# Feed-forward products of a two-layer encoder as seven block products instead of eight, with weight sums on GpSimd

## The chip, the cores and the metric

The kernel runs on one core of a Trainium2 chip. The metric is the device time of one execution in microseconds (us); three executions of the kernel before were timed. TensorE (PE) multiplies matrices out of SBUF into the banks of PSUM (8 banks of 128 x 512 float32), VectorE (DVE), ScalarE (ACT) and GpSimd (POOL) work elementwise, and the queue of SyncE (SP) issues loads. Each engine runs its own instructions in their order and waits on semaphores for the others.

## What is computed

Two layers of an encoder over 512 tokens of 1024 features. Each layer has a feed-forward at half weight, three token mixers in parallel with one output projection, and a second feed-forward:

```python
D_MODEL = 1024; SEQ = 512; DEPTH = 2; D_FF = 2816

def swiglu(x, wg, wu, wd):
    return (jax.nn.silu(x @ wg) * (x @ wu)) @ wd

for l in range(DEPTH):
    x = x + 0.5 * swiglu(rms_norm(x, ffn1_norm[l]), ffn1_wg[l], ffn1_wu[l], ffn1_wd[l])
    h = rms_norm(x, mix_norm[l])
    ...                                   # differential, dilated and latent attention on h @ w_in[l]
    x = x + mix @ w_o[l]
    x = x + 0.5 * swiglu(rms_norm(x, ffn2_norm[l]), ffn2_wg[l], ffn2_wu[l], ffn2_wd[l])
```

All inputs are float32. The change touches the four feed-forwards, and with them how x is held.

## The kernel before

**Products.** Every float32 operand is split in two parts of the type float32r: the high part `hi` is a rounded copy made by ScalarE (L69), the low part `lo` is what is left, made by VectorE (L70: the raw tile less the high part, both in SBUF). A product is three matmuls (`mm3`, L81 to L83): hi x hi, hi x lo, lo x hi.

**Layout.** x is held with features on partitions (`xT`, eight tiles of 128 x 512). A feed-forward splits x times the norm's gain into `xg` (eight pairs of tiles, L72 and L73); the token factor of the norm is applied behind the products, as a row `rb` that L200 makes.

**Feed-forward.** The 2816 hidden features are 22 columns of 128, taken in groups of 2, 4, 4, 4, 4, 4 (`FF_GROUPS`). `gate_up` (L232) makes one column: 24 matmuls for the gate into a bank of A, 24 for the up part into a bank of B, each with a 128 x 128 weight as the stationary and 512 tokens as the moving operand. VectorE and ScalarE make silu(gate) x up of them (L245 to L250) and split it. `down` (L256) multiplies a group by the rows of `wd`, eight times 12 matmuls into banks of D, and adds half of each to x (L264). The down products of a group are issued between the columns of the next group. Weights come through SP's queue into two `raw` tiles of 8 KB a partition (tag `raw`, `N_RAW` = 2), high and low parts into four tiles each (`N_W` = 4).

**POOL** adds the squares for the norm at each border (L184, L186), makes powers (L98) and works in the mixers (L442, L802).

**Order.** The program's text gives an order; a scheduler places the instructions of each engine but SP by its own estimate, so neighbouring columns mix on PE and DVE. SP's loads stay in the order of the text (`manual_schedule`).

## Time and profile before

| what | value |
|---|---|
| timed executions, median of 3 | 2065.02 us (2064.61 to 2065.61) |
| span of the profiled execution, first to last instruction | 2064.5 us |
| PE busy, share of the span | 98% |
| DVE, ACT, POOL busy | 58%, 42%, 18% |
| mean granted clock of PE, share of full | 0.997 |
| loads and stores, mean over the span | 93 GB/s |
| one feed-forward (1036 to 1398 us) | 362 us |
| one mixer (391 to 676 us) | 285 us |

How to read it: the profiled execution has its span as its own time, and the timed ones lie 0.1 to 1.1 us above it. A matmul's shown duration overlaps the next one's, so PE's pace is read from a stretch's length and count. An operation's duration on DVE or POOL includes time in which it is issued but can't go on. Busy shares are averages over stages; the stage tables say more.

### The profile page before, as it was taken

Reading aid. Unit: us, or ns where it says so; the run is one execution under the profiler, and the core shown is the slowest. Engines: PE = TensorE matmul, PEld = TensorE weight load, DVE = VectorE, ACT = ScalarE, POOL = GpSimd, SP = SyncE. Lnnn points to the kernel's source line nnn. Section 1 sums busy time; section 2 is a strip of 40 time slices with the busy share of each in tenths; the row PEclk is TensorE's granted clock in tenths of the full one; section 3 lists DMA queues with packets and bytes.
Section 4 is the critical chain, followed back from the end, with each engine's and each line's share of the span. In section 5 each row is a group of like instructions: output and inputs, shape, how many; then the busy total and the mean of one; then the engine's idle time right before and its main releaser. Section 6 shows DMA issues by size and latency. Waiting matters only on the chain.

```text
span 2064.5 us, 27177 instructions
## 1 busy us (share of the span) xinstructions
PE 2032.4 (98%) x10535; PEld 1732.5 (84%) x10535; DVE 1204.3 (58%) x2043; ACT 876.2 (42%) x1547; POOL 380.4 (18%) x442
## 2 busy tenths in 40 slices
PE   8999999999999999999999999999998999999999
PEld 6788888999888888888888888889997888888887
DVE  5544454678897655444555544455879985445444
ACT  5222232567876332222333222235779763223221
POOL 2100000444683100000010000005547630000000
PEclk9999999999999999999999999999999999999999
DMA  4632232421111233322323332234211022333322
GB/s 142 213 123 82 82 103 92 114 81 49 48 58 59 79 117 108 107 82 82 103 76 118 104 111 82 82 102 122 63 37 57 30 88 88 102 93 112 102 82 82
DMA packets 192689, 188.82 MB, mean 91 GB/s; under 512 B 8303, under 2 KB 187557, under 8 KB 192560
## 3 DMA queue, kind: packets, MB, share of 16 engines
q1 hardware_dynamic: 183200, 170.02, 26.5%
q10 hardware_dynamic: 7104, 11.27, 1.8%
q0 software_dynamic: 2256, 5.78, 0.9%
...
## 4 chain that ended last, share of the span: by engine, by line
PE 90%; DVE 4%; ACT 3%; DMA 2%; issue 1%; SPq 0%; ACTq 0%; POOL 0%; DVEq 0%; POOLq 0%
PE psA L83 12%; PE psA L81 12%; PE psA L82 12%; PE psB L82 8%; PE psB L81 8%; PE psB L83 8%; PE psD L81 7%; PE psD L83 7%; PE psD L82 7%; PE psD L810 2%; DMA raw<-in_ffn_wg_dram 2%; PE psE L839 1%; PE psE L830 1%; PE psC L429 1%; PE psB L505 1%; DVE wlo L70 1%
## 5 line engine op out<-in xcount | busy, mean ns | idle before, releaser
L69 ACT ACTIVATE whi<-raw 128x1024 fp32r<-128x1024 f32 (+3 forms) x448 | 362.8, 814 | 883.7 <-PE psB L82 287.8
L70 DVE TENSOR_TENSOR wlo<-raw,whi 128x1024 fp32r<-128x1024 f32 (+3 forms) x448 | 423.6, 948 | 119.7 <-ACT whi L69 110.5
L83 PE MATMUL psA<-xg,wlo 128*128 128x512 f32 x800 | 313.8, 392 | 3.5 <-DVE wlo L70 3.5
L81 PE MATMUL psA<-xg,whi 128*128 128x512 f32 x800 | 313.7, 392 | 1.6 <-ACT whi L69 1.6
L82 PE MATMUL psA<-xg,whi 128*128 128x512 f32 x800 | 312.6, 391 | 0.0
L82 PE MATMUL psB<-xg,whi 128*128 128x512 f32 x736 | 286.5, 389 | 0.0
L83 PE MATMUL psB<-xg,wlo 128*128 128x512 f32 x736 | 286.5, 389 | 0.0
L81 PE MATMUL psB<-xg,whi 128*128 128x512 f32 x736 | 286.5, 389 | 0.0
L81 PE MATMUL psD<-a,whi 128*128 128x512 f32 x704 | 274.4, 391 | 1.0 <-DVE xT L264 1.0
L83 PE MATMUL psD<-a,wlo 128*128 128x512 f32 x704 | 274.1, 389 | 0.0
L249 DVE TENSOR_TENSOR qk<-psB,o 128x512 f32<-128x512 f32 x88 | 60.8, 691 | 290.2 <-PE psB L83 290.2
L264 DVE SCALAR_TENSOR_TENSOR xT<-psD,xT 128x512 f32<-128x512 f32 x192 | 132.1, 690 | 142.4 <-PE psD L83 142.4
L184 POOL COPY o<-qk 128x512 f32<-128x512 f32 x5 | 4.2, 838 | 988.8 <-ACT qk L181 988.8
L83 PEld LDWEIGHTS psA<-xg,wlo 128*128 128x128 f32 x800 | 150.8, 188 | 37.3 <-DVE wlo L70 6.1
L81 PEld LDWEIGHTS psA<-xg,whi 128*128 128x128 f32 x800 | 151.0, 189 | 32.9 <-ACT whi L69 2.3
L82 PEld LDWEIGHTS psA<-xg,whi 128*128 128x128 f32 x800 | 150.9, 189 | 30.9
L81 PE MATMUL psA<-whi,xg 128*128 128x256 f32 (+2 forms) x592 | 173.8, 294 | 1.6 <-ACT xg L72 0.8
L82 PE MATMUL psA<-wlo,xg 128*128 128x256 f32 (+2 forms) x592 | 170.1, 287 | 0.0
L83 PE MATMUL psA<-whi,xg 128*128 128x256 f32 (+2 forms) x592 | 170.1, 287 | 0.0
L81 PEld LDWEIGHTS psB<-xg,whi 128*128 128x128 f32 x736 | 138.1, 188 | 28.9
L82 PEld LDWEIGHTS psB<-xg,whi 128*128 128x128 f32 x736 | 138.2, 188 | 28.6
L83 PEld LDWEIGHTS psB<-xg,wlo 128*128 128x128 f32 x736 | 138.1, 188 | 28.6
...
## 6 DMA issues: line engine op xcount, KB each, us to landing
...
```

Of the source, the lines that this page charges most:

```text
L69: nc.scalar.activation(hi, src, AF.Copy)
L70: eng.tensor_tensor(out=lo, in0=src, in1=hi.bitcast(F32), op=ALU.subtract)
L81: nc.tensor.matmul(o, ah, bh, start=(i == 0), stop=False)
L82: nc.tensor.matmul(o, ah, bl, start=False, stop=False)
L83: nc.tensor.matmul(o, al, bh, start=False, stop=(i == n - 1))
L249: nc.vector.tensor_tensor(out=tu, in0=pU, in1=rb[0], op=ALU.mult)
L264: nc.vector.scalar_tensor_tensor(out=xT[d], in0=pY, scalar=0.5, in1=xT[d], op0=ALU.mult, op1=ALU.add)
L429: nc.tensor.transpose(pt[:rows, t * P:(t + 1) * P], zsel(t), ident)
L505: nc.tensor.matmul(pS, qk[c, 0][:96, t * P:(t + 1) * P], qk[c, 1][:96, :], start=True, stop=True)
L810: nc.tensor.transpose(pT[:, kt * P:(kt + 1) * P], e[:, kt * P:(kt + 1) * P], ident)
L830: nc.tensor.matmul(hd.av[:, t * 64:(t + 1) * 64], pt[:, kt * P:(kt + 1) * P], hd.v(kt), start=(kt == 0), stop=(kt == NT - 1),)
L839: nc.tensor.matmul(o, hd.v(kt), x[:, :, kt, :], start=(i + kt == 0), stop=(i == 1 and kt == NT - 1))
```

## The change

The feed-forwards go by one Strassen level in Winograd's form. Tokens, the features summed over and the outputs are each cut in two, so a product of 2 x 2 blocks takes seven block products and sums in place of eight block products.

- x is held with tokens on partitions (`X`, eight tiles of 128 x 512). Stationary operands are now 128 tokens of x or of the hidden values, and weights are the moving operand, up to 512 columns wide. PE transposes x (`x_transposed`) and the hidden values (`hidden_operand`) into the operand's layout: 32 and 88 transposes in a feed-forward.
- For each 128 of the summed features the operand has eight pieces of 256 tokens: the blocks A11, A12, A21, A22 and four sums S1 to S4. `sums` makes the sums on POOL in three instructions (512, 256 and 256 elements), `split7` makes the high and low parts of seven pieces (1792 elements).
- An up block covers n columns (2, then five times 4). Its second operand is the gate's (11 and 21, by halves of the features) and the up part's weights (12 and 22). A down block is `wd` for the same n columns, cut by halves of columns and of outputs. `Seven` holds either. It loads eight raw tiles of 128 x 2 x 512 for an up block of four, four for a down block. POOL makes the four sums of weights: u1 = 11 + 12, then in place 12 + 22, u1 + 22 and 21 = (u1 + 22) + 21: for an up block of four two adds of 128x1024 each, for a down block one each.
- `run` issues seven products, below called first to seventh: (A11, 11) and (A12, 21) into banks of A, (S1, u1) into D, (S2, u1 + 22) and (S3, 12 + 22) into B, (S4, 22) on top of D, (A22, 21) into A. Each has two token tiles: for an up block of four 24 matmuls of 512 columns, for a down block 12. Between the products of a bank the sum so far is read by `done`: ScalarE copies q1, VectorE reads q6, q5 and the others out of PSUM; in a down block POOL adds q6 and q67 to x (three additions per token tile).
- Order of blocks: up 0, up 1, down 0, up 2, down 1, ... up 5, down 4, down 5. Behind the second product of up i come the transposes, sums and splits of the operand for down i - 1.
- The raw ring has ten tiles of 4 KB a partition. Mixers read x by transposes and add the output projection to it with tokens on partitions; its first half goes in 192 matmuls of 256 columns in place of 96 of 512. The store of x at the end needs no transposes.

The core of the diff (the mixers' adaptions and the readers of q1, q12 are left out):

```diff
-FF_GROUPS = (2, 4, 4, 4, 4, 4)
+FF_BLOCKS = (2, 4, 4, 4, 4, 4)
...
-    N_XG, N_A, N_RAW, N_W, N_QK = 16, 6, 2, 4, 8
+    N_XG, N_A, N_RAW, N_W, N_QK, N_T = 16, 6, 10, 4, 8, 5
...
+    X = [[cp.tile([P, H], F32, name=f"x{t}{d}") for d in range(2)] for t in range(NT)]
...
+    I_A11, I_A12, I_S2, I_S3, I_S1, I_S4, I_A22, I_A21 = range(8)
+    def sums(c, eng=nc.gpsimd):
+        eng.tensor_tensor(
+            out=c[:, I_S3:I_S1 + 1, :], in0=c[:, I_A21:I_A21 + 1, :].to_broadcast([P, 2, Q]),
+            in1=c[:, I_A11:I_A22 + 1:I_A22, :], op=ALU.subtract,
+        )
+        eng.tensor_tensor(out=c[:, I_S2, :], in0=c[:, I_A11, :], in1=c[:, I_S1, :], op=ALU.subtract)
+        eng.tensor_tensor(out=c[:, I_S4, :], in0=c[:, I_A12, :], in1=c[:, I_S2, :], op=ALU.subtract)
+    class Seven:
...
+        def add(self, dst, a, b):
+            for h in range(len(self.parts)):
+                if (dst, h) not in self.raw:
+                    self.raw[dst, h] = wraw([P, len(self.parts[h]), self.w])
+                nc.gpsimd.tensor_tensor(out=self.raw[dst, h], in0=self.raw[a, h], in1=self.raw[b, h], op=ALU.add)
+        def multiply(self, i, key, tag, start, stop):
+            w = []
+            for h, ks in enumerate(self.parts):
+                hi, lo = wsplit(self.raw[key, h], [P, len(ks), self.w])
+                w += [(hi[:, j, :], lo[:, j, :]) for j in range(len(ks))]
+            for t in range(2):
+                if start:
+                    self.banks[tag, t] = bank(tag)
+                tk = slice(t * P, (t + 1) * P)
+                mm3(
+                    self.banks[tag, t][:, :self.w], [(h[:, i, tk], lo[:, i, tk]) for h, lo in self.ops], w,
+                    start, stop,
+                )
+                yield t, self.banks[tag, t][:, :self.w]
+        def run(self, done):
+            self.add("u1", "11", "12")
+            for t, o in self.multiply(I_A11, "11", "A", True, False):
+                done("q1", t, o)
+            for t, o in self.multiply(I_A12, "21", "A", False, True):
+                done("q12", t, o)
+            self.add("12", "12", "22")
+            yield
+            for t, o in self.multiply(I_S1, "u1", "D", True, False):
+                done("q5", t, o)
+            self.add("u1", "u1", "22")
+            for t, o in self.multiply(I_S2, "u1", "B", True, False):
+                done("q6", t, o)
+            self.add("21", "u1", "21")
+            for t, o in self.multiply(I_S3, "12", "B", False, True):
+                done("q67", t, o)
+            for t, o in self.multiply(I_S4, "22", "D", False, True):
+                done("q53", t, o)
+            for t, o in self.multiply(I_A22, "21", "A", True, True):
+                done("q4", t, o)
...
+        def split7(op, c):
+            h, lo = op
+            nc.scalar.activation(h, c[:, :7, :], AF.Copy)
+            nc.vector.tensor_tensor(out=lo, in0=c[:, :7, :], in1=h.bitcast(F32), op=ALU.subtract)
...
-        def gate_up(m, raws, aT):
-            i = m % 2
-            c = slice(i * P, (i + 1) * P)
-            rg, ru = raws
-            gh, gl = wsplit(rg[:, :, c], [P, KD, P])
-            pG = bank("A")
-            mm3(pG, [(gh[:, k, :], gl[:, k, :]) for k in range(KD)], xg)
-            uh, ul = wsplit(ru[:, :, c], [P, KD, P])
-            pU = bank("B")
-            mm3(pU, [(uh[:, k, :], ul[:, k, :]) for k in range(KD)], xg)
...
-        def down(m0, gn, aT, final):
-            for dp in range(KD // 2):
-                rw = wload(wd[:, m0:m0 + gn, 2 * dp * P:2 * (dp + 1) * P], [P, gn, 2 * P])
...
-                    d = 2 * dp + i
-                    dh, dl = wsplit(rw[:, :, i * P:(i + 1) * P], [P, gn, P])
-                    pY = bank("D")
-                    mm3(pY, [(dh[:, j, :], dl[:, j, :]) for j in range(gn)], aT)
-                    nc.vector.scalar_tensor_tensor(
-                        out=xT[d], in0=pY, scalar=0.5, in1=xT[d], op0=ALU.mult, op1=ALU.add
-                    )
...
+                elif what == "q5":
+                    s["q5", t] = o
+                elif what == "q6":
+                    s["v", t] = hid[:, t, :w]
+                    nc.vector.tensor_tensor(out=s["v", t], in0=o, in1=s["q1", t][:, :w], op=ALU.subtract)
+                elif what == "q67":
+                    y = s["w", t] = s["q1", t][:, :w]
+                    nc.vector.tensor_tensor(out=y, in0=o, in1=y, op=ALU.subtract)
+                    nc.vector.tensor_tensor(out=hid[:, u, :w], in0=s["q5", t], in1=y, op=ALU.add)
+                elif what == "q53":
+                    y = hid[:, t, :w]
+                    nc.vector.tensor_tensor(out=y, in0=o, in1=y, op=ALU.add)
+                    nc.vector.scalar_tensor_tensor(
+                        out=y, in0=y, scalar=r[:, t:t + 1], in1=s["g", t][:, :w], op0=ALU.mult, op1=ALU.mult
+                    )
+                else:
+                    y = s["w", t]
+                    nc.vector.tensor_tensor(out=y, in0=o, in1=y, op=ALU.subtract)
+                    nc.scalar.activation(y, y, AF.Silu, scale=r[:, u:u + 1])
+                    z = hid[:, u, :w]
+                    nc.vector.scalar_tensor_tensor(
+                        out=z, in0=z, scalar=r[:, u:u + 1], in1=y, op0=ALU.mult, op1=ALU.mult
+                    )
...
+                elif what in ("q6", "q67"):
+                    y = tmp() if what == "q6" else s["q1", t]
+                    nc.vector.scalar_tensor_tensor(
+                        out=y, in0=o, scalar=0.5, in1=s["q1", t], op0=ALU.mult, op1=ALU.subtract
+                    )
+                    if what == "q6":
+                        nc.gpsimd.tensor_tensor(out=X[t][1], in0=X[t][1], in1=y, op=ALU.add)
+                    else:
+                        nc.gpsimd.tensor_tensor(out=X[u][1], in0=X[u][1], in1=y, op=ALU.add)
+                        nc.gpsimd.tensor_tensor(out=X[u][0], in0=X[u][0], in1=y, op=ALU.subtract)
...
+        def start_down(i):
+            downs[i] = down(*blocks[i])
+            turn(i)
+        run_up(0, lambda: None)
+        for i in range(1, nb):
+            run_up(i, lambda: start_down(i - 1))
+            run_down(i - 1, (lambda: start_down(i)) if i == nb - 1 else (lambda: None))
+        run_down(nb - 1)
```

How it moves instructions. POOL in the kernel before, at the border of the first feed-forward and the first mixer (`o` is the sum of squares, `r` the token factor, `zn` a head's normed queries or keys). Inside a feed-forward, apart from setup's loads in the first, POOL has nothing.

```order
L186 TENSOR_TENSOR o_2795<-o_2795,qk_2809 128x512
L186 TENSOR_TENSOR o_2795<-o_2795,qk_2812 128x512
L186 TENSOR_TENSOR o_2795<-o_2795,qk_2815 128x512
L98 TENSOR_TENSOR r_2823<-r_2823,nhalf 128x4
L485 TENSOR_TENSOR rsd_2827<-rsd_2827,nhalf 128x8x2 x2
```

POOL in the kernel after, from the last two weight sums of a down block (raw_1724 to raw_1732 are its tiles, raw_1732 is its u1) to the sums of the next up block (raw_1881 to raw_1900, u1 in raw_1898 and raw_1900); `c_385` and `c_388` are the operand of the next down block, `t` are q6 and q67 of this one.

```order
L194 TENSOR_TENSOR raw_1732<-raw_1732,raw_1730 128x1024
L194 TENSOR_TENSOR raw_1728<-raw_1732,raw_1728 128x1024
L168 TENSOR_TENSOR c_385_1982<-c_385_1982 128x512
L194 TENSOR_TENSOR raw_1898<-raw_1881,raw_1885 128x1024
L172 TENSOR_TENSOR c_385_1982<-c_385_1982 128x256
L322 TENSOR_TENSOR x_74<-x_74,t_1807 128x512
L194 TENSOR_TENSOR raw_1900<-raw_1883,raw_1887 128x1024
L194 TENSOR_TENSOR raw_1885<-raw_1885,raw_1893 128x1024
L322 TENSOR_TENSOR x_76<-x_76,t_1817 128x512
L168 TENSOR_TENSOR c_388_2000<-c_388_2000 128x512
L173 TENSOR_TENSOR c_385_1982<-c_385_1982 128x256
L194 TENSOR_TENSOR raw_1887<-raw_1887,raw_1895 128x1024
```

Behind these come four additions to x, two more sums of c_388, then the adds in place on u1 (raw_1898, raw_1900) and 21: the weight sums of three loads, the sums of the operand and the additions to x now share one queue.

DVE in the kernel before, two columns of a feed-forward: low parts of weights (`wlo`), and the gate and up parts out of banks A and B.

```order
L245 TENSOR_TENSOR qk_1543<-psA_1489,o_281 128x512
L70 TENSOR_TENSOR wlo_1628<-raw_1623,whi_1627 128x1024
L249 TENSOR_TENSOR qk_1547<-psB_1518,o_281 128x512
L250 TENSOR_TENSOR qk_1547<-qk_1547,qk_1545 128x512
L70 TENSOR_TENSOR wlo_1657<-raw_1625,whi_1656 128x1024
L70 TENSOR_TENSOR v_283_1551<-qk_1547,a_1550 128x512
L245 TENSOR_TENSOR qk_1612<-psA_1558,o_281 128x512
L70 TENSOR_TENSOR wlo_1697<-raw_1623,whi_1696 128x1024
```

DVE in the kernel after, where an up block ends and its down block begins (psA_1692, psA_1708 are the up block's seventh product, psD_1559 the sixth; raw_1724, raw_1728 and raw_1732 are the down block's 11, 21 and u1):

```order
L64 TENSOR_TENSOR wlo_1735<-raw_1724,whi_1734 128x1024
L293 TENSOR_TENSOR t_1443<-psA_1692,t_1443 128x512
L296 SCALAR_TENSOR_TENSOR hid_1417<-hid_1417,r_232,t_1443 128x512
L64 TENSOR_TENSOR wlo_1757<-raw_1728,whi_1756 128x1024
L287 TENSOR_TENSOR hid_1417<-psD_1559,hid_1417 128x512
L293 TENSOR_TENSOR t_1458<-psA_1708,t_1458 128x512
L64 TENSOR_TENSOR wlo_1776<-raw_1732,whi_1775 128x1024
L288 SCALAR_TENSOR_TENSOR hid_1417<-hid_1417,r_232,t_1494 128x512
L296 SCALAR_TENSOR_TENSOR hid_1417<-hid_1417,r_232,t_1458 128x512
L305 SCALAR_TENSOR_TENSOR x_73<-psA_1738,x_73 128x512
```

DVE somewhat later, from the low parts of the next up block's 21 (raw_1889, raw_1891) to those of its u1 (raw_1898, raw_1900) and 12 + 22 (raw_1885):

```order
L64 TENSOR_TENSOR wlo_1941<-raw_1889,whi_1940 128x1024
L305 SCALAR_TENSOR_TENSOR x_76<-psD_1787,x_76 128x512
L64 TENSOR_TENSOR wlo_1945<-raw_1891,whi_1944 128x1024
L248 TENSOR_TENSOR s_382_1979<-c_385_1982,s_381_1978 128x1792
L305 SCALAR_TENSOR_TENSOR x_77<-psA_1865,x_77 128x512
L305 SCALAR_TENSOR_TENSOR x_79<-psA_1873,x_79 128x512
L248 TENSOR_TENSOR s_384_1981<-c_388_2000,s_383_1980 128x1792
L64 TENSOR_TENSOR wlo_2019<-raw_1898,whi_2018 128x1024
L64 TENSOR_TENSOR wlo_2023<-raw_1900,whi_2022 128x1024
L64 TENSOR_TENSOR wlo_2055<-raw_1898,whi_2054 128x1024
L64 TENSOR_TENSOR wlo_2059<-raw_1900,whi_2058 128x1024
```

The low part of the down block's u1 (wlo_1776) stands behind the up block's last bank, and the low parts of the next up block's u1 (wlo_2019, wlo_2023) behind the splits of both operand tiles.

## Rows read from the trace of the kernel before

**Rows 1.** The page, part 1: busy us, share of the span, instructions.

```profile
PE 2032.4 (98%) x10535; PEld 1732.5 (84%) x10535; DVE 1204.3 (58%) x2043; ACT 876.2 (42%) x1547; POOL 380.4 (18%) x442
```

**Rows 2.** Stretches: length, busy us of each engine, PEclk, DMA share, GB/s.

```profile
core 0: us, PE busy (x) PEld busy (x) DVE busy (x) ACT busy (x) POOL busy (x), PEclk, DMA share, GB/s
391.00:676.00 285.00, 278.78 (x1991) 257.44 (x1990) 223.96 (x503) 204.31 (x452) 156.81 (x182) 0.99 0.21 64
676.00:1036.00 360.00, 358.30 (x1584) 295.79 (x1583) 184.02 (x244) 111.78 (x153) 12.69 (x10) 1.00 0.30 97
1036.00:1398.00 362.00, 361.20 (x1598) 298.51 (x1597) 181.41 (x243) 112.17 (x154) 12.30 (x9) 1.00 0.31 96
398.00:404.00 6.00, 6.00 (x52) 6.00 (x52) 2.20 (x5) 1.81 (x5) 2.75 (x1) 1.00 0.56 172
```

**Rows 3.** Chain that ended last: start, us, what; four transposes.

```profile
2046.00 0.44 PE psC L290 x4
```

**Rows 4.** Lines L186, L442 of POOL: ns min/median/max, first and last start.

```profile
L186 POOL TENSOR_TENSOR o<-o,qk x35: 1293/1522/1832, 370.0 to 1699.3; 128x512 f32<-128x512 f32 x35
...
L442 POOL TENSOR_TENSOR zn<-zd,rsd x96: 397/406/1475, 407.0 to 1496.3; 128x128 f32<-128x128 f32 x96
L442 POOL TENSOR_TENSOR zn<-zl,rsl x48: 613/622/1312, 482.5 to 1565.0; 128x256 f32<-128x256 f32 x48
```

**Rows 5.** Timeline of DVE inside a feed-forward: start, us, what.

```profile
199.41 0.68 DVE L70 TENSOR_TENSOR wlo<-raw,whi 128x512 fp32r<-128x512 f32 x1
201.52 0.69 DVE L264 SCALAR_TENSOR_TENSOR xT<-psD,xT 128x512 f32<-128x512 f32 x1 [1.43 <-PE psD L83]
202.40 1.23 DVE L70 TENSOR_TENSOR wlo<-raw,whi 128x1024 fp32r<-128x1024 f32 x1 [0.18 <-ACT whi L69]
```

**Rows 6.** Groups by form, ScalarE: busy us, mean ns | idle before.

```profile
L69 ACT ACTIVATE whi<-raw 128x1024 fp32r<-128x1024 f32 x208 | 218.9, 1059 | 359.1 <-PE psB L82 105.0 <-PE psA L82 78.2 <-DMA raw<-in_ffn_wu_dram 67.6
L69 ACT ACTIVATE whi<-raw 128x512 fp32r<-128x512 f32 x192 | 120.3, 630 | 457.8 <-PE psB L82 156.4 <-PE psA L82 147.4 <-PE psD L82 147.3
L72 ACT ACTIVATE xg<-xT,gT 128x512 fp32r<-128x512 f32 x48 | 33.8, 716 | 12.9 <-DVE xT L264 12.9
L69 ACT ACTIVATE pt<-psD 128x512 fp32r<-128x512 f32 x96 | 56.2, 596 | 17.1 <-PE psD L810 16.0 <-DVE zq L707 0.6
```

**Rows 7.** Timeline of DVE, then POOL, at a feed-forward's end.

```profile
378.89 0.74 DVE L73 SCALAR_TENSOR_TENSOR xg<-xT,gT,xg 128x512 fp32r<-128x512 f32 x1
379.55 0.68 DVE L264 SCALAR_TENSOR_TENSOR xT<-psD,xT 128x512 f32<-128x512 f32 x1
380.15 1.71 DVE L70 TENSOR_TENSOR wlo<-raw,whi 128x1024 fp32r<-128x1024 f32 x1
381.79 1.78 DVE L73 SCALAR_TENSOR_TENSOR xg<-xT,gT,xg 128x512 fp32r<-128x512 f32 x1
...
379.12 1.67 POOL L186 TENSOR_TENSOR o<-o,qk 128x512 f32<-128x512 f32 x1 [1.24 <-ACT qk L181]
381.65 1.37 POOL L186 TENSOR_TENSOR o<-o,qk 128x512 f32<-128x512 f32 x1 [0.87 <-ACT qk L181]
```

**Rows 8.** Timeline of DVE, then POOL, at a mixer's end.

```profile
667.89 1.79 DVE L73 SCALAR_TENSOR_TENSOR xg<-xT,gT,xg 128x512 fp32r<-128x512 f32 x1
669.60 1.77 DVE L70 TENSOR_TENSOR wlo<-raw,whi 128x512 fp32r<-128x512 f32 x1
671.29 1.77 DVE L73 SCALAR_TENSOR_TENSOR xg<-xT,gT,xg 128x512 fp32r<-128x512 f32 x1
...
667.46 5.05 POOL L186 TENSOR_TENSOR o<-o,qk 128x512 f32<-128x512 f32 x3 [0.22 <-ACT qk L181]
```

**Rows 9.** Timeline of PE in the first feed-forward: start, us, what [wait].

```profile
98.13 0.50 PE L81 MATMUL psA<-xg,whi 128*128 128x512 f32 x1 [1.49 <-ACT whi L69]
99.39 0.50 PE L83 MATMUL psA<-xg,wlo 128*128 128x512 f32 x1 [0.52 <-DVE wlo L70]
...
101.00 0.63 PE L82 MATMUL psA<-xg,whi 128*128 128x512 f32 x1
101.43 0.63 PE L83 MATMUL psA<-xg,wlo 128*128 128x512 f32 x1
```

**Rows 10.** Stretches behind these waits; columns as in rows 2.

```profile
99.30:101.30 2.00, 1.92 (x6) 1.59 (x7) 1.11 (x3) 1.57 (x2) 0.00 (x0) 0.73 0.00 0
101.30:103.30 2.00, 2.00 (x6) 1.52 (x6) 2.00 (x3) 2.00 (x3) 0.00 (x0) 0.50 0.00 0
103.30:105.30 2.00, 2.00 (x10) 1.60 (x9) 2.00 (x3) 0.02 (x1) 0.00 (x0) 0.92 0.16 29
```

406 lines of the change are left out of this document (219 added, 187 removed).

## The prediction

> **What bounds the kernel now.** First the page's busy shares [rows 1], then the table of stretches [rows 2]: the tensor engine (PE) is busy 98% of a span of 2064.5 us, and in a feed-forward stretch of 360 us it issues 1584 matmuls, 360/1584 = 0.227 us each. That is its own pace: a feed-forward has 22 x 2 x 8 x 3 + 22 x 8 x 3 = 1584 products of 512 columns, and nothing else fits in. VectorE (DVE) is busy 184 of the 360 us, ScalarE (ACT) 112, GpSimd (POOL) 13. So PE alone sets the time of the four feed-forwards (some 362 us each, 1448 us of the span); the rest is two mixers of some 285 us and the ends. The three runs have a median of 2065.02 us, 0.5 above the span; I sum against the span, and the 0.5 is lost in my errors.
>
> **What the change takes from PE.** Seven block products in place of eight. In a feed-forward: five up blocks of four columns with 168 matmuls of 512 columns, one of two with 168 of 256 columns; down 5 x 84 + 42 of 512. That is 1302 x 0.227 + 168 x 0.12 (52 of 256 columns fill 6.00 us [rows 2]) = 316 us, against 360: 44 saved. Added: 88 transposes of hidden tiles and 32 of x, four in 0.44 us [rows 3], 0.11 each: 13 us; the old kernel has 80 such in all. PE alone would gain 4 x (44 - 13) + 9 = some 130 us: about 1940.
>
> **What it gives to the others.** Take the steady pair: one up block (four columns) and the down block of the block before, 168 + 84 matmuls and 16 transposes: 59 us of PE.
> POOL does 12 adds of weights (128x1024), 6 sums of the operand (two of 512, four of 256 elements), 6 updates of x (512). A plain add of two 512-element inputs takes 1.29 us when undisturbed (the least of 35), a product with a broadcast input 0.40 at 128 and 0.61 at 256 [rows 4]. Through a start of 0.18 us this is 2.17 ns an element, so 2.40 us at 1024, which no row shows; bounds are 1.29 + 512 x 1.69 ns = 2.16 (the slope of the broadcast rows) and 2 x 1.29 = 2.59. I take 2.40, by the add's own row. Sum: 28.8 + 5.5 + 7.7 = 42 us a pair.
> The Trainium skill's GPSIMD Engine Reference (3.1 Elementwise) gives 4497 ns for a float32 add of 2048, which would make a 1024 some 2.25 us as an estimate, 2 us less a pair and 40 us less in all; no run here has that size.
> DVE does 21 low parts of weights (128x1024, 1.23 us undisturbed, 0.68 at 512 [rows 5]), two of 1792 elements (by the same two rows 2.05) and four 512-element products out of SBUF (0.75): 33 us with both inputs in SBUF. 22 operations of 0.69 read one input from PSUM: 15 us. Sum 48. ACT: 21 high parts of 1.06, two of 1.70 (1.06 at 1024 and 0.63 at 512 carried on to 1792) and twelve copies of some 0.6 [rows 6]: 33 us. Each by itself stays below 59.
>
> **Why they don't fit side by side.** At the end of a feed-forward in the old kernel POOL adds while DVE works [rows 7]. The low part at 380.15 lasts 1.71, not 1.23: it got going 0.48 late, 0.16 before the POOL add that began at 379.12 ends. The one at 381.79 lasts 1.78, not 0.74, behind the add at 381.65. The operation at 379.55, whose one input is in PSUM, takes its 0.68 under the same add. From 667.89 on [rows 8] three DVE operations of two SBUF inputs take turns with three adds, 1.70 us a turn, which is 1.29 + 0.71 less 0.30. So a POOL operation and a DVE operation with two SBUF inputs exclude each other, and each handover gives back about 0.15 us. In a pair 42 + 33 = 75 us exclude each other; were all 22 to 27 of them sandwiched, some 8 us come back: 67 to 75 us, against PE's 59. The gain is gone by this alone.
> The Trainium skill's page SBUF — State Buffer (Who interferes with whom) calls it a lock held for the whole instruction, with the other side fully blocked. The rows agree but for the 0.15 us at each handover; by the page's words a pair would cost 3 us more than I get below and the kernel some 65 us more.
>
> **The order makes it worse.** In the POOL order shown the down block's second use of u1 (row raw_1732<-raw_1732,raw_1730) needs DVE's low part of u1, and in DVE's order that stands behind the subtraction from the up block's last bank (t_1458<-psA_1708), that is, behind the end of PE's up block. Call this end E. POOL runs in order, so all that stands behind it waits too: 18 operations until the last sum of the operand (c_388). Behind that sum ACT splits 1792 elements, then DVE, and only behind these, in DVE's order, come the low parts of u1 for the next up block's third product (wlo_2019, wlo_2023). PE has the down block (19 us) and two products (11 us) for that time.
> From E to the third product: DVE 0.69 + 1.23 = 2.0 with signals; POOL 6 x 2.40 + 5.5 + 7.7 = 27.7; between them eight low parts, two products and one split of DVE, 8 x 1.23 + 1.5 + 2.05 = 13.4 less 11 x 0.30 = 10.1; then 1.70 + 2.05 + 1.23 = 5.0: **45 us**, of which PE fills 30.
> From the third product to the next E: PE 5 x 5.45 = 27.3, and waits: u1+22 is added in place once u1 is split, 2 x 2.40, then 1.06, then the low part behind the add of 21, up to 2.4 + 1.23, so the fourth product ends at about 13.7 in place of 10.9; the fifth waits for DVE to read the banks (q6), which stands behind low parts that wait for two more adds, some 4 us: **35 us** in all. POOL stands still for 15 of these.
> A pair: **80 us**, where PE has 59. Its clock: after waits of 1.49 and 0.52 us PE ran 3.4 us at 0.50 of its clock, the 1.2 GHz level, and lost 2 x (0.27 + 0.50 + 0.08) = 1.7 us [rows 9, 10]. Waits of 15 us will do so in each pair; most of that falls where u1+22 is late anyhow, so I count it at nothing, and at 1.7 us a pair in rival (c).
>
> **The sum of a feed-forward.** Three full pairs 240; the pair with the small down block 76 (four adds and four low parts at half size). Start to the end of the first up block 45: POOL's 11 us of x sums, 10 of adds at half size, some 10 of DVE operations that exclude them, then five products of 2.9. Second up block 43 (PE 38, and 5 for u1+22). The last two down blocks 47: POOL from E on 5 + 5.5 + 7.7 + 4.8 + some 12 of DVE, then the seventh product and x. 45 + 43 + 76 + 240 + 47 = 451, against 362: +89, four times **+356**. Each mixer: 32 transposes of x (3.5 us), the first half of the output projection 192 x 0.12 for 96 x 0.227 (+1), two more steps at each border: +7, twice 14. The first feed-forward has setup's loads and waits in POOL's queue between adds: +8; x comes behind 2 MB of weights: +5. The end loses transposes and gains a wait for POOL: nothing. 2064.5 + 356 + 27 = 2447.5, say **2450 us**. DMA is no term: 6.3 MB a pair in 80 us is 79 GB/s, and these stretches move 96 to 97 now at a share of 0.3 [rows 2].
>
> **Rivals.** (a) The other side: PE stays the bound. Were the adds and low parts to slip into each other's gaps and loads come early enough, the 130 us would show, less some 8 us of filling at each feed-forward and the 27: about 1990. It decides where the excluded sum of a pair falls below 59 us: adds of 1024 at 1.1 us would do it. The add's own row [rows 4] speaks against it. (b) The exclusion counts, the order doesn't: POOL runs ahead of E, and a feed-forward costs its excluded time, 5 x 67 + 37 + 14 and 15 at its ends, 401: 2064.5 + 4 x 39 + 27 = 2248. For it: POOL stands still for 15 us a pair, so work could be there; against it the order itself. (c) All of the forecast, and a spell at half clock that counts in each of 24 up blocks, 24 x 1.7 = 41, and no handover gives anything back, 3.3 us in each of 20 pairs: 66; together 2555, say 2560.
>
> **How the numbers follow.** Forecast 2450: 0.58. (c) 2560: 0.16. (b) 2248: 0.17. (a) 1990: 0.08. No change at all: 0.01. The adds' bounds, 2.16 to 2.59, move a pair by 12 x 0.2 = 2.5 us, the kernel by some 55. The range reaches to (b) and just past (c), 2230 to 2580, and leaves out (a). A difference of 0.2% (4 us) is about what can be told from none: faster 0.08, same 0.01, slower 0.91.
>
> **What would show it.** POOL busy some 1300 us (247 in each feed-forward, 310 in the mixers) and more with waits inside, and its adds of 1024 at 2.4 us or more by the median, up to 3.6 where a low part stood in front. DVE's low parts of 1024 well above 1.23 on average, 1.6 to 2.2, its operations out of PSUM still 0.69. PE busy below 85%, its longest waits in front of products into psD (the third) put down to wlo or whi, and behind those a granted clock below 1. A period of 80 us from one up block's end to the next. If the low parts stay at 1.23, the exclusion is wrong; if they are long and the period is 67 to 70, the order is; if PE stays above 95%, all of it is.

## The result, and the profile after

The changed kernel takes 2548.47 us (median of four, 2546.9 to 2548.82), the kernel before 2065.32 us on the same chip (median of four): a ratio of 1.2337, 95% interval 1.2319 to 1.2356. One of the four executions of the kernel before took 4496.43 us and is left out of the ratio. The profiled execution spans 2544.8 us, 480.3 more than the 2064.5 before. The forecast was 2450, its range 2230 to 2580.

The page of the changed kernel, part 1, against [rows 1]:

```profile
PE 2050.2 (81%) x10695; PEld 1719.3 (68%) x10695; DVE 1926.8 (76%) x2305; ACT 1217.4 (48%) x1927; POOL 1560.6 (61%) x1014
```

PE is no longer the bound: 19% of the span it stands still. Its busy time has not fallen either, at a mean granted clock of 0.908 where it was 0.997. Stretches of the changed kernel, columns as in [rows 2]: first feed-forward, mixer, the second and third feed-forward, mixer:

```profile
17.00:492.50 475.50, 363.94 (x1578) 291.41 (x1577) 365.58 (x331) 194.07 (x231) 306.06 (x164) 0.88 0.27 80
492.50:801.80 309.30, 289.48 (x2129) 268.36 (x2128) 229.81 (x519) 209.77 (x470) 162.25 (x186) 0.98 0.24 72
801.80:1278.60 476.80, 369.25 (x1628) 297.42 (x1627) 367.33 (x310) 198.17 (x245) 306.03 (x151) 0.89 0.24 73
1278.60:1752.90 474.30, 362.36 (x1592) 291.06 (x1591) 363.66 (x306) 197.73 (x246) 310.26 (x154) 0.88 0.25 75
1752.90:2057.70 304.80, 288.22 (x2130) 267.86 (x2129) 228.98 (x519) 211.24 (x471) 157.76 (x182) 0.98 0.22 63
```

A feed-forward has some 475 us where it had 360 to 362, a mixer 305 to 309 where it had 285. By these stretches the two mixers make 44 of the 480 us, and the four feed-forwards with the start and the end the other 436.

The groups by form (busy us, mean ns of one, idle before): DVE's low parts and POOL's sums of weights:

```profile
L64 DVE TENSOR_TENSOR wlo<-raw,whi 128x1024 fp32r<-128x1024 f32 x468 | 879.8, 1894 | 134.9 <-ACT whi L63 131.3 <-DMA raw<-in_ffn_wg_dram 2.4
L194 POOL TENSOR_TENSOR raw<-raw,raw 128x1024 f32<-128x1024 f32 x240 | 683.8, 2860 | 494.7 <-DVE wlo L64 488.4 <-DMA raw<-in_ffn_wd_dram 3.2
...
L305 DVE SCALAR_TENSOR_TENSOR x<-psA,x 128x512 f32<-128x512 f32 x96 | 65.3, 683 | 76.9 <-POOL x L325 75.6 <-PE psA L78 1.3
```

The low part that took 1.23 us alone [rows 5] has a mean of 1.89; an operation with one input in PSUM keeps its 0.68.

Now one pair, from the end of one up block to the end of the next. DVE's read of the last bank (L293) marks the ends. The rows are, in this order: DVE at the first end; PE's wait for its next first product and the start of its third; POOL's last updates of x and DVE's reads of bank A that hold PE up; the low part of u1; DVE at the second end:

```profile
1144.66 0.68 DVE L293 TENSOR_TENSOR t<-psA,t 128x512 f32<-128x512 f32 x1
...
1181.52 0.77 PE L76 MATMUL psA<-whi,s 128*128 128x512 f32 x1 [16.52 <-DVE x L305]
1192.43 0.39 PE L76 MATMUL psD<-whi,s 128*128 128x512 f32 x1
...
1179.39 1.26 POOL L325 TENSOR_TENSOR x<-x,t 128x512 f32<-128x512 f32 x1
1181.83 1.27 POOL L325 TENSOR_TENSOR x<-x,t 128x512 f32<-128x512 f32 x1
...
1180.68 0.69 DVE L305 SCALAR_TENSOR_TENSOR x<-psA,x 128x512 f32<-128x512 f32 x1 [2.37 <-POOL x L325]
1189.63 1.23 DVE L64 TENSOR_TENSOR wlo<-raw,whi 128x1024 fp32r<-128x1024 f32 x1 [1.23 <-ACT whi L63]
...
1227.11 0.68 DVE L293 TENSOR_TENSOR t<-psA,t 128x512 f32<-128x512 f32 x1
```

The period is 1227.11 - 1144.66 = 82.45 us (81.2, 81.5 and 82.5 in this feed-forward; forecast 80). PE waits 16.52 us, for the bank of A that the down block's seventh product still holds: DVE may read it only when POOL has updated the same tile of x. The four pieces of the pair, columns as above:

```profile
1144.70:1164.80 20.10, 19.86 (x94) 15.81 (x92) 18.91 (x18) 10.56 (x14) 14.66 (x7) 1.00 0.25 73
1164.80:1181.50 16.70, 0.20 (x1) 0.01 (x1) 10.70 (x8) 3.04 (x3) 16.70 (x9) 0.66 0.11 39
1181.50:1187.00 5.50, 5.48 (x13) 4.34 (x14) 1.33 (x2) 1.70 (x1) 3.03 (x4) 0.50 0.01 3
1187.00:1227.10 40.10, 38.19 (x165) 30.26 (x164) 34.60 (x24) 17.12 (x19) 23.18 (x8) 1.00 0.27 85
```

Behind the wait PE runs 5.5 us at a granted clock of 0.50 (1.2 GHz), which costs it half of that, 2.75 us. So 82 us are the forecast's 59 of work, 16.5 + 2 of waits, 2.75 of clock and some 2 of small change.

### The profile page after: what moved, and what is told of

Read it like the earlier page. It is cut to its first block, busy times and chain, and to the rows that moved or that the text cites. A ratio compares the mean times of both kernels' runs of the same rounds, so it can differ in the third digit from the quotient of the medians.

```text
span 2544.8 us, 29288 instructions
## 1 busy us (share of the span) xinstructions
PE 2050.2 (81%) x10695; PEld 1719.3 (68%) x10695; DVE 1926.8 (76%) x2305; ACT 1217.4 (48%) x1927; POOL 1560.6 (61%) x1014
## 4 chain that ended last, share of the span: by engine, by line
PE 36%; POOL 23%; DVE 21%; issue 12%; ACT 6%; DMA 1%; SPq 0%; ACTq 0%; POOLq 0%; DVEq 0%
DVE wlo L64 12%; POOL raw L194 11%; PE psA L76 7%; PE psA L77 6%; PE psA L78 6%; ACT whi L63 3%; POOL x L322 2%; POOL c L168 2%; POOL x L324 2%; PE psB L76 2%; PE psB L77 2%; DVE x L305 2%; PE psB L78 2%; POOL c L172 2%; DVE hid L296 2%
## 5 line engine op out<-in xcount | busy, mean ns | idle before, releaser
L194 POOL TENSOR_TENSOR raw<-raw,raw 128x1024 f32<-128x1024 f32 (+1 forms) x288 | 756.9, 2639 | 599.7 <-DVE wlo L64 571.8
L64 DVE TENSOR_TENSOR wlo<-raw,whi 128x1024 fp32r<-128x1024 f32 (+2 forms) x566 | 974.9, 1736 | 157.9 <-ACT whi L63 154.1
L63 ACT ACTIVATE whi<-raw 128x1024 fp32r<-128x1024 f32 (+2 forms) x566 | 548.8, 984 | 566.5 <-PE psB L78 269.5
L76 PE MATMUL psA<-whi,s 128*128 128x512 f32 (+1 forms) x840 | 348.0, 419 | 301.8 <-DVE x L305 270.5
L76 PEld LDWEIGHTS psA<-whi,s 128*128 128x128 f32 x840 | 173.1, 206 | 347.6 <-issue 292.0
L77 PE MATMUL psA<-wlo,s 128*128 128x512 f32 (+1 forms) x840 | 338.8, 404 | 0.9 <-DVE wlo L64 0.9
L78 PE MATMUL psA<-whi,s 128*128 128x512 f32 (+1 forms) x840 | 336.1, 401 | 0.0
L76 PE MATMUL psB<-whi,s 128*128 128x512 f32 (+1 forms) x560 | 216.1, 400 | 52.5 <-DVE hid L280 36.9
L76 PE MATMUL psD<-whi,s 128*128 128x512 f32 (+1 forms) x560 | 212.0, 397 | 57.2 <-ACT whi L63 35.9
L76 PE MATMUL psA<-whi,xg 128*128 128x256 f32 (+3 forms) x752 | 223.8, 298 | 19.4 <-DVE xg L67 5.9
L77 PE MATMUL psA<-wlo,xg 128*128 128x256 f32 (+3 forms) x752 | 220.9, 294 | 0.1
L78 PE MATMUL psA<-whi,xg 128*128 128x256 f32 (+3 forms) x752 | 220.8, 294 | 0.0
L78 PE MATMUL psB<-whi,s 128*128 128x512 f32 (+1 forms) x560 | 216.6, 389 | 0.3 <-DVE s L370 0.3
L78 PE MATMUL psD<-whi,s 128*128 128x512 f32 (+1 forms) x560 | 215.7, 390 | 1.1 <-DVE s L370 1.1
L78 PEld LDWEIGHTS psA<-whi,s 128*128 128x128 f32 x840 | 171.5, 205 | 34.7
```

Of the source, the lines that this page charges most:

```text
L63: nc.scalar.activation(hi, src, AF.Copy)
L64: eng.tensor_tensor(out=lo, in0=src, in1=hi.bitcast(F32), op=ALU.subtract)
L76: nc.tensor.matmul(o, ah, bh, start=(start and i == 0), stop=False, **kw)
L77: nc.tensor.matmul(o, ah, bl, start=False, stop=False, **kw)
L78: nc.tensor.matmul(o, al, bh, start=False, stop=(stop and i == n - 1), **kw)
L194: nc.gpsimd.tensor_tensor(out=self.raw[dst, h], in0=self.raw[a, h], in1=self.raw[b, h], op=ALU.add)
```

## Experiments

Each run was timed in three rounds beside the kernel before (2066.0 to 2066.7 us). A period is the distance between two ends of full up blocks inside a feed-forward, the border that from the last up block's end of a feed-forward to the first one's end of the next: 81.2 to 82.6 and 107 us in the changed kernel.

### Is the exclusion the price?

```diff
# free_lo, in wsplit
-        split(h, lo, src)
+        if zero and len(shape) == 3 and ffn_on:
+            nc.scalar.activation(h, src, AF.Copy)
+            z = zero[-1][:, None, :shape[2]].to_broadcast(list(shape))
+            nc.vector.tensor_tensor(out=lo, in0=src, in1=z, op=ALU.subtract)
...
```

Here `zero` is a bank of PSUM that holds zeros.

> In the feed-forwards DVE's low parts of weights subtract a bank of PSUM filled with zero (read with step 0 over the two halves) instead of the high part in SBUF: the same operation and length with one input in SBUF, so by the forecast's rule POOL's additions do not exclude it. That leaves the low parts equal to the whole weight, and drops their wait for ACT. The transposes of hidden values use one bank in place of two. Theory of the exclusion: low parts of 1024 go from a mean of 1.89 to 1.2 to 1.4 us, POOL's additions from 2.86 to 2.35 to 2.45; behind an up block's end POOL needs 2 + 6 x 2.35 + 4 + 7.6 = 28 us to the last update of x, so the wait for bank A falls from 16.5 to about 8 and the period to 70 to 74 us; kernel 2548 - 20 x 9 - 4 x 5 = 2350 us, 2300 to 2400. Rival, the operations are slow for a reason of their own (memory, type) and do not exclude each other: means stay, the period stays at 81 us, the kernel within 1% of 2548 us.

2267.89 us, ratio 1.0972 (1.0956 to 1.0989): 281 us faster than the changed kernel, period 68.2, wait for bank A 3.5. The groups by form of this run, then a pair of the changed kernel and one of this run, columns as above:

```profile
L163 DVE TENSOR_TENSOR wlo<-raw,psE 128x1024 fp32r<-128x1024 f32 x420 | 507.0, 1216 | 188.2 <-PE psA L77 84.0 <-PE psD L77 71.0 <-PE psB L77 13.5
L201 POOL TENSOR_TENSOR raw<-raw,raw 128x1024 f32<-128x1024 f32 x240 | 606.3, 2542 | 414.1 <-DVE wlo L163 343.5 <-ACT whi L161 65.7 <-DMA raw<-in_ffn_wd_dram 1.9
...
1063.20:1144.70 81.50, 62.99 (x270) 50.21 (x269) 63.77 (x51) 32.23 (x35) 52.41 (x24) 0.90 0.26 78
952.53:1020.53 68.00, 62.56 (x269) 50.54 (x268) 48.97 (x51) 32.25 (x36) 43.28 (x24) 0.95 0.30 92
```

The same operation with one input moved to PSUM takes 1.216 in place of 1.894 us, and POOL's additions 2.54 in place of 2.86. So the two do exclude each other, and without it a pair is some 13 us shorter. The period and the kernel came out below my ranges, the kernel 80 us below what I expected: PE's clock over a pair is 0.95 here and 0.90 in the changed kernel, which I had not counted; whether the wait for ACT that the low parts lost has a share in the 13 us was not separated. The low parts' length does not hang on that wait: in no_adds and dma_adds, the next two runs, both of their inputs are in SBUF and they wait for ACT as before, but POOL makes no sums of weights; their mean is 1.35 and 1.32 us. The Trainium skill's page SBUF — State Buffer (Who interferes with whom) says that a VectorE instruction with at most one SBUF input, outside its two-port modes, doesn't contend with GpSimd; these 1.216 us agree.

### Are the additions the price?

```diff
# no_adds
-                    self.raw[dst, h] = wraw([P, len(self.parts[h]), self.w])
-                nc.gpsimd.tensor_tensor(out=self.raw[dst, h], in0=self.raw[a, h], in1=self.raw[b, h], op=ALU.add)
+                    self.raw[dst, h] = self.raw[a, h]
```

> POOL's sums of weights are left out (288 additions): the products take the loaded tiles as they are, and u1 is the tile of 11. Everything else stays. Theory of the chain with POOL and DVE excluding each other: POOL keeps 13 us a pair, the excluded sum is 46 us, PE with its 59 us is the bound: period 59 to 63 us, PE over 93% busy in a feed-forward's middle; with 20 pairs of 20 us less and some 12 us less at each feed-forward's ends 2548 - 400 - 50 = 2100 us, between 2050 and 2140, since the mixers' 25 us each stay. Rival, DVE's own 48 us or the banks hold PE back: the period stays above 68 us and the kernel above 2230 us.

2201.19 us, ratio 1.0653 (1.0637 to 1.0669), period 64.7, border 90. Both expectations missed: the pairs came to 2 us above my range, and the kernel 60 above. PE still waited for the bank of A, 82 us in 18 waits. Taking the additions away gives back 347 us of the 483, not all of them. It also leaves u1 without tiles of its own, so that more of the ring is free; what that gives was not separated. The low parts of this run, then of the next, dma_adds:

```profile
L64 DVE TENSOR_TENSOR wlo<-raw,whi 128x1024 fp32r<-128x1024 f32 x468 | 630.1, 1354 | 197.4 <-ACT whi L63 188.8 <-DMA raw<-in_ffn_wd_dram 5.5
...
L64 DVE TENSOR_TENSOR wlo<-raw,whi 128x1024 fp32r<-128x1024 f32 x468 | 612.4, 1320 | 338.8 <-ACT whi L63 329.1 <-DMA raw<-in_ffn_wu_dram 6.2 <-DMA raw<-in_ffn_wd_dram 2.1
```

```diff
# dma_adds
-                    self.raw[dst, h] = wraw([P, len(self.parts[h]), self.w])
-                nc.gpsimd.tensor_tensor(out=self.raw[dst, h], in0=self.raw[a, h], in1=self.raw[b, h], op=ALU.add)
+                    self.raw[dst, h] = wload(self.load(int(a[0]) - 1, int(a[1]) - 1, self.parts[h]), [P, len(self.parts[h]), self.w])
+                nc.gpsimd.dma_start(self.raw[dst, h], self.raw[a if dst == b else b, h], accum_op=ALU.add)
```

> The sums of weights are made by accumulating transfers that POOL's queue issues, from SBUF into SBUF, and u1 starts as a second load of 11 or, for a down block, likewise: POOL's 12 additions a pair become 12 transfers of 512 KB and 3 more loads. If an accumulating transfer costs what a plain one does, 6.3 + 7.9 = 14.2 MB in some 62 us are 229 GB/s; a stretch of the trace moved 208 GB/s at a share of 0.70, so the share would be 0.77 and PE the bound: period 60 to 66 us, kernel 2080 to 2200 us. Rival, an accumulating transfer takes twice the engines' time or a latency of some 10 us each in the chain u1 = 11 + 12, u1 + 22, + 21: transfers become the bound, period 80 us or more, kernel 2550 us or more. What POOL needs to issue one is in no trace so far; bounds 0 and the 2.35 us of the addition it replaces.

2396.94 us, ratio 1.1597 (1.1578 to 1.1616), period 73.3: between theory and rival. The transfers are not the bound (share 0.79 in a pair at 198 GB/s), but a sum of 1024 now takes 5.4 us (median) from issue to landing, and POOL waits 325 us in all for an earlier one before it can issue the next.

### Is it the order?

```diff
# q4_bank
-            for t, o in self.multiply(I_A22, "21", "A", True, True):
+            for t, o in self.multiply(I_A22, "21", self.last, True, True):
...
-            return Seven([operand() for _ in range(n // 2)], load, n // 2, H)
+            return Seven([operand() for _ in range(n // 2)], load, n // 2, H, "B")
```

`self.last` is "B" in a down block and stays "A" in an up block.

> One word is changed: the seventh product of a down block goes into a bank of B instead of a bank of A, so that the next up block's first product no longer waits for a bank that DVE reads only behind POOL's updates of x (the 16.5 us wait that stands ahead of each full up block in the trace). Theory of the chain (forecast): two things come late nearly together, the bank of A 36.9 us behind the up block's end and the low part of u1 for the third product some 46 us behind it (1189.63 + 1.23 in the trace, against 1144.66). With the bank gone PE waits two products later; the period goes from 81.5 to 79 to 81 us and the kernel to 2490 to 2550 us. Rival, the wait is what the trace's label says and nothing else: the 16.5 us go, the period falls to 64 to 67 us, the kernel to some 2548 - 20 x 16 = 2230 us.

2519.81 us, ratio 1.2192 (1.2167 to 1.2217): 29 us faster, period 78 to 80. The 16.5 us ahead of the first product are gone, and almost as much has come back elsewhere. PE's waits of the whole run (us, times, longest):

```profile
PE psB L76 <- ACT whi L63: 95.7, 19, 9.4
PE psB L76 <- DVE hid L280: 77.4, 39, 7.6
PE psA L77 <- DVE wlo L64: 41.1, 29, 2.0
PE psB L77 <- DVE wlo L64: 37.4, 25, 2.9
```

So the wait that the trace names was the first of several that end almost together; the high and low parts of the next weights and DVE's reads of bank B stand right behind it. Part of the waits in front of B may be of the edit's own making, since the seventh product now shares that bank; this was not separated.

```diff
# dve_adds
-                nc.gpsimd.tensor_tensor(out=self.raw[dst, h], in0=self.raw[a, h], in1=self.raw[b, h], op=ALU.add)
+                nc.vector.tensor_tensor(out=self.raw[dst, h], in0=self.raw[a, h], in1=self.raw[b, h], op=ALU.add)
```

> The sums of weights move from POOL to DVE; nothing else changes. An addition of 1024 out of SBUF takes DVE some 1.23 us as the low part does, where POOL takes 2.35. DVE then has 48 + 12 x 1.23 = 63 us a pair, POOL 13, and what excludes each other is 33 + 15 + 13 = 61. Theory of the exclusion: DVE becomes the bound with 63 us and some handovers, and DVE's low parts fall to a mean of 1.25 to 1.45; the period is 66 to 72 us, the kernel 2548 - 20 x 12 - 4 x 8 = 2280, between 2230 and 2350. Rival, the order alone made it slow: the chain behind the up block's end stays and shrinks by 6 x 1.1 us only, period 74 to 76, kernel 2400 to 2440.

2487.99 us, ratio 1.2043 (1.2025 to 1.2061): the period stays at 79 to 81, and both expectations missed. The low parts did fall to a mean of 1.37, as the exclusion has it, but the time did not follow: my number was the one for a bound by DVE's total, and this is none. One pair of this run in two stretches, up to PE's first product and from there on:

```profile
1033.80:1070.70 36.90, 19.88 (x94) 15.94 (x92) 36.81 (x32) 15.08 (x17) 24.48 (x12) 0.85 0.19 57
1070.70:1114.50 43.80, 42.49 (x176) 34.60 (x177) 28.89 (x30) 16.82 (x18) 0.43 (x1) 0.94 0.33 97
```

DVE (third of the busy times) works through the first 36.9 us without a pause and then has 15 to spare. Its queue there, with the read of bank A behind both splits of the operand and the low parts of the next blocks:

```profile
1066.93 3.08 DVE L248 TENSOR_TENSOR s<-c,s 128x1792 fp32r<-128x1792 f32 x1
1069.93 0.68 DVE L305 SCALAR_TENSOR_TENSOR x<-psA,x 128x512 f32<-128x512 f32 x1
1071.17 0.69 DVE L305 SCALAR_TENSOR_TENSOR x<-psA,x 128x512 f32<-128x512 f32 x1 [0.56 <-POOL x L325]
1078.87 1.23 DVE L64 TENSOR_TENSOR wlo<-raw,whi 128x1024 fp32r<-128x1024 f32 x1 [7.01 <-ACT whi L63]
```

Here the next low part could be made from 1071.9 on, and PE takes the one for its third product only some 10.9 us behind 1070.8, so that here, unlike in the changed kernel, the bank is late alone. That gave the next run, dve_q4, which has the edits of dve_adds and q4_bank:

> The run dve_adds (sums of weights on DVE, 2488 us, period 80 us) with a bank of B for a down block's seventh product. In dve_adds DVE works without a pause for 37 us from the up block's end (1033.8) to the read of bank A (1071.2 + 0.7) that lets PE's next first product go at 1070.8, and PE waits 16.8 us. Theory of the queue's order: both operand splits are done by 1070.0 there, so the low part for the third product could follow at 1071 to 1072, while PE now takes it at 1081.6, after two products; so here the two late things are 10 us apart, and without the bank's wait the period falls by about 9 to 69 to 72 us, the kernel to 2488 - 20 x 9 = 2308, between 2280 and 2350. Rival, as on the changed kernel itself (q4_bank, 3 us a pair): period 76 to 78 us, kernel 2415 to 2450.

2314.48 us, ratio 1.1211 (1.1192 to 1.1229), period 69 to 71: 173 us from one bank, with the same instructions. This is as expected, and q4_bank's 29 us beside it show that a wait is worth what the next late thing leaves.

The in-place sum was my own candidate for POOL's standing still:

```diff
# own_v1
-            self.add("u1", "u1", "22")
+            self.add("v1", "u1", "22")
...
-            self.add("21", "u1", "21")
+            self.add("21", "v1", "21")
```

> The sum u1 + 22 gets a tile of its own instead of being made in place, so POOL no longer waits for DVE to have made the low part of u1 (16.9 us of POOL standing still ahead of each up block's end in the trace, and 6.3 us in the next block). All adds and low parts stay, the ring of ten tiles too, of which one more per half is now held. Theory of the order (forecast): with POOL free to run ahead of the up block's end a pair comes down towards its excluded time, 67 to 75 us, and the kernel to 2548 - 20 x 7 to 14 = 2270 to 2410. Rival: it is not the order but the tiles: with one more held the loads of the next block start later and POOL waits for them instead; the period stays at 79 to 84 us, the kernel at 2520 to 2600.

2530.19 us, ratio 1.2245 (1.2226 to 1.2263), period 78.4 to 78.6, the last of each feed-forward 81 to 85: the rival's time. POOL does make the down block's sums earlier, but now stands 12.7 us ahead of the up block's end, and again elsewhere, without a releaser in the trace. POOL's waits in one pair of this run:

```profile
POOL raw L194 <- issue: 25.3, 2, 12.7
POOL raw L194 <- DVE wlo L64: 15.0, 2, 7.7
```

A tile more in the ring was to show whether it is the ring:

```diff
# own_v1_11, beside the edits of own_v1
-    N_XG, N_A, N_RAW, N_W, N_QK, N_T = 16, 6, 10, 4, 8, 5
+    N_XG, N_A, N_RAW, N_W, N_QK, N_T = 16, 4, 11, 4, 8, 4
```

> The run own_v1 (a tile of its own for u1 + 22, 2530 us, period 78.6 us) with a ring of eleven tiles in place of ten; to make room a feed-forward has four temporary tiles in place of five and a mixer four tiles of scores in place of six. In own_v1 POOL's first addition for the next up block still stands 12.7 us ahead of the up block's end, in a wait that the trace does not name. Theory of the ring: it waits for a free tile, and with one more it starts earlier: period 70 to 76 us, kernel 2400 to 2490. Rival, it waits for something that eleven tiles do not change (the loads' order, or DVE's queue): period 77 to 80 us, kernel 2510 to 2560.

2551.21 us, ratio 1.2344 (1.2325 to 1.2362), period 82 to 85, longer than either expectation, the kernel within the rival's range: it isn't cured by one tile, and the fewer temporary tiles may cost something. What POOL waits for there stays open.

### What do the borders cost?

```diff
# x_sums_dve
-            sums(c)
+            sums(c, nc.vector)
```

The line stands where x's operand is made; the sums of the hidden operand stay on POOL.

> Only the four operand sums of x at each feed-forward's start (12 instructions) move from POOL to DVE. In the trace of after the border from the last up block's end to the first one's end of the next feed-forward is 107 us where the forecast had 92. Theory: the border is a chain of x's last updates, transposes, sums and splits, in which 11 us of sums on POOL stand among its additions; on DVE they take about half: border 100 to 104 us, kernel 2548 - 4 x 5 = 2528, between 2515 and 2540. Rival: the sums are hidden behind the first products, and POOL's additions of weights set the border: 106 to 108 us, kernel within 6 us of 2548.

2515.82 us, ratio 1.2179 (1.2161 to 1.2197): the border falls to 102.7, the periods stay at 80.5 to 82.6; 33 us in all, more than four times the border's 4.3. The same sums stand at every feed-forward's start: the first up block of all ends 10.2 us earlier than in the changed kernel (59.05 for 69.23), and from a feed-forward's last up block's end across a mixer to the next first one's end it is 4.7 and 4.6 us less.

The run no_adds together with both edits, q4_bank and x_sums_dve, shows what is left when the sums of weights are left out and the bank is free:

> The run no_adds (POOL's sums of weights left out, 2201 us, period 64.7 us) with the bank of B for a down block's seventh product and with x's operand sums on DVE: all that the sums, the bank and POOL's part at a feed-forward's start cost is gone. Theory: PE is the bound in the pairs, period 60 to 61 us, the border from the last up block's end to the first one's end of the next feed-forward 84 to 88 us in place of 90; kernel 2201 - 20 x 4 - 4 x 4 = 2105, between 2080 and 2130, so above the kernel before even so, because the starts and ends of the stages cost more than the fewer products save. Rival, the forecast's case in which PE is the bound throughout: 1990, up to 2040 us.

2109.65 us, ratio 1.0210 (1.0195 to 1.0225). A pair, then the border in two pieces, then a feed-forward from one last up block's end to the next:

```profile
891.00:951.60 60.60, 59.79 (x270) 48.54 (x269) 48.35 (x50) 31.47 (x36) 20.24 (x12) 1.00 0.34 105
1012.20:1056.00 43.80, 38.91 (x164) 29.90 (x163) 35.95 (x37) 19.86 (x24) 22.14 (x14) 0.92 0.14 38
1056.00:1097.70 41.70, 33.49 (x222) 29.38 (x221) 34.11 (x59) 29.61 (x57) 7.47 (x5) 0.96 0.35 113
1012.17:1374.38 362.21, 343.31 (x1592) 279.40 (x1591) 287.80 (x320) 193.20 (x244) 113.99 (x70) 0.98 0.32 98
```

The pair is PE's own 60. But a feed-forward is 362.2 us (85.6 the border, then 38.6, 56.3 and three times 60.6), what it was before [rows 2]: the fewer products save, and the transposes, the border and the waits eat all of it. With the sums of weights at nothing the kernel is still 2% slower.

### All that helped, with every sum kept

dve_q4 with x's sums on DVE and a down block's sums by the transfers of dma_adds:

```diff
# mix_q4_xs, in add, beside the edits of dve_q4 and x_sums_dve
+                if self.last == "B":
...
+                    nc.gpsimd.dma_start(self.raw[dst, h], self.raw[a if dst == b else b, h], accum_op=ALU.add)
+                    continue
```

> Everything that helped, with all sums kept: an up block's sums of weights on DVE, a down block's by accumulating transfers that POOL's queue issues, a bank of B for a down block's seventh product, x's operand sums on DVE. Theory: in dve_q4 (2314 us) DVE is the bound, busy without a pause for some 56 of 71 us; four of its twelve additions less take 4 x 1.23 = 5 us off it, and no POOL addition stands beside it: period 62 to 66 us against 69 to 71, the border some 95 us against 99; kernel 2314 - 20 x 5 - 4 x 5 = 2195, between 2150 and 2240. It does not come near the kernel before, as the run with no sums at all has 2110. Rival, what DVE's queue is late with is set by PE and ACT behind the up block's end and not by DVE's total: period 68 to 70 us, kernel 2270 to 2320.

2299.34 us, ratio 1.1128 (1.1109 to 1.1146), period 68.2, border 102.8: the rival's number. Five us less of DVE's work bring the period down by one to three, which fits the rival: what DVE is late with follows the up block's end and not DVE's total. The run dma_q4 has the edits of dma_adds and q4_bank alone:

> The accumulating transfers in place of POOL's additions (the run dma_adds, 2397 us, period 73.3 us) together with the bank of B for a down block's seventh product. In dma_adds the wait for the bank of A was 7.3 us for each of 23 up blocks. Theory of the tie: the low part for the third product is nearly as late, so that 1 to 4 us a pair go: kernel 2300 to 2380 us, and PE's waits stand in front of products into B and D. Rival, with additions off POOL the bank is what is left alone: all 7 us go, period 66 us, kernel 2230 to 2260.

2350.10 us, ratio 1.1386 (1.1367 to 1.1406), period 68: 5.3 us a pair, a little over what I gave the tie, the kernel within its range. No version beat the kernel before.

## Why the prediction was right, and where its steps failed

**The likeliest case was the one that came.** The signs it named: low parts between 1.6 and 2.2 (1.89), operations out of PSUM at 0.69 (0.68), PE below 85% (81%), a period of 80 (81 to 82.5). Additions of 1024 at "2.4 or more by the median": an undisturbed one took 2.34 to 2.40, the mean is 2.86, the longest 4.15. POOL's busy time came to 1561, 1300 and the waits inside. One sign failed: PE's longest waits stand in front of the first product, and not of the third. One feed-forward against the sum, from the end at 1227.11 to that at 1701.36; the rows are the ends of its six up blocks (1227.11, shown above, is the end of the last one before):

```profile
1334.07 0.41 DVE L293 TENSOR_TENSOR t<-psA,t 128x256 f32<-128x256 f32 x1
1379.91 0.68 DVE L293 TENSOR_TENSOR t<-psA,t 128x512 f32<-128x512 f32 x1
1455.38 0.68 DVE L293 TENSOR_TENSOR t<-psA,t 128x512 f32<-128x512 f32 x1
1537.00 0.68 DVE L293 TENSOR_TENSOR t<-psA,t 128x512 f32<-128x512 f32 x1
1618.77 0.68 DVE L293 TENSOR_TENSOR t<-psA,t 128x512 f32<-128x512 f32 x1
1701.36 0.68 DVE L293 TENSOR_TENSOR t<-psA,t 128x512 f32<-128x512 f32 x1
```

| step | forecast | measured |
|---|---|---|
| last up block's end to the next feed-forward's first product | 47 | 62.8 |
| to the first up block's end | 45 | 44.2 |
| second up block | 43 | 45.8 |
| pair with the small down block | 76 | 75.5 |
| three full pairs | 240 | 246.0 |
| sum | 451 | 474.3 |
| all the rest of the kernel, beyond before | 27 | 31 |

**The step that was mis-sized is the tail**, 47 for 62.8. I gave POOL 35 us behind E and let the seventh product and x follow in 12. PE's rows of it, ScalarE's copy of the last down block's first product (L311), the first product of the next feed-forward, and the stretch from the third product to the first transposes of x:

```profile
1253.88 1.22 PE L76 MATMUL psD<-whi,s 128*128 128x512 f32 x2 [6.12 <-ACT whi L63]
1257.74 0.79 PE L77 MATMUL psD<-wlo,s 128*128 128x512 f32 x1 [2.64 <-DVE wlo L64]
...
1263.79 0.60 ACT L311 ACTIVATE t<-psA 128x512 f32<-128x512 f32 x1 [0.34 <-PE psA L78]
...
1289.87 0.58 PE L76 MATMUL psA<-whi,s 128*128 128x256 f32 x1 [4.13 <-ACT c L367]
...
1253.90:1278.60 24.70, 22.06 (x85) 17.46 (x86) 19.82 (x21) 7.23 (x9) 20.67 (x11) 0.83 0.18 45
```

The last down block's operand is ready only 26 (high parts) to 28 us (low parts) behind E, and its third product, which the scheduler put first, starts at 26.8. All seven products of the block, 84 matmuls, are then still to come: ScalarE copies the first one's bank at 1263.79. They take 24.7 us up to the first transposes of x at 1278.6, 19 of them work at full clock and the rest a wait of 2.6 and a spell at half clock. Then x's transposes wait for its last update and the first product for the operand (11.3 us). POOL's chain was sized well (36.5 us to its last sum of weights for this block); what PE has behind it, a whole block and not one product, was not.

How the 97 us by which the span exceeds my 2447.5 divide, by the ends of the up blocks in the trace: 37 lie between the first and the last end inside the four feed-forwards (366.4 to 370.0 us each, where the terms give 359), 15 at this border, 69 from the last end across a mixer to the next first one (422.1 and 415.1, where the terms give 47 + 285 + 7 + 45 = 384); start and end together have 127.5, where the terms and the 46.5 of the kernel before give 151.5, so 24 less. The 69 hold the tail again, but also what the mixers cost beyond the 7 us each that I gave them; the runs don't separate the two. That the line of the rest came out at 31 for 27 is luck: what the mixers cost more, the start and the end cost less.

**The chain's place was partly wrong, its length right.** I had the wait in front of the third product, for the low part of u1, 45 us behind E, and 35 from there to the next E. The third product started 1192.43 - 1144.66 = 47.8 behind E, and the rest took 34.7. But PE waited at the first product, for the bank of A, which I had overlooked. q4_bank shows that this wait hid the others and added little (29 us in all). So the forecast of the period stood on two chains of nearly equal length, of which I knew one; that the other was not longer was luck.

**The exclusion.** In the chain I counted 10.1 us of low parts taking turns with POOL; free_lo gives 13 us a pair, with the clock and the lost wait for ACT in it. The mechanism is shown, and its size is of the right order; whether 10.1 was too little can't be told from this.

**The clock** I counted at nothing in the forecast and at 1.7 us a pair in rival (c). The rows show 2.75 behind a wait of 16.5 us, about as much as the 2 us by which I had each of the three full pairs too short. (c) with its 2560 is nearer to 2548 than the forecast, but its sum is not what was measured: the larger half of it was handovers in the pairs, which were right to 2 us, and it had nothing for the tail.

**Rival (a)**, 1990 with PE as the bound, was wrong beyond its chance: no_adds_q4_xs is that case with the sums at nothing, and it takes 2110. The term is the 8 us of filling for a feed-forward: 362.2 us stand against the forecast's 316 + 13 = 329 of PE's own work, 33 where I had 8. PE stands still for 362.2 - 343.3 = 19 of them, 13 at the border alone (85.5 - 72.4), and is busy for 14 more than I priced, partly below full clock (0.92 and 0.96 at the border). Outside the feed-forwards 2105.7 - 4 x 362.2 = 657 us stand against 2064.5 - 4 x 361 = 620, 37 where I had 27. That the mixers' part of this is the wait for x and its transposes at their edges is not shown.

**Rival (b)**, 2248 with the order unbound, was not reached by freeing POOL from u1's low part (own_v1). Moving the sums to DVE took most of the exclusion away and left the period at 80, and a bank then took 10 us from it; and with the exclusion gone but the sums still on POOL (free_lo) the period is 68.2, where PE alone needs 60.6. So the order binds by itself, as forecast, though through a bank and DVE's queue as much as through POOL's.
